# Reciprocal norms spread by transposes of their own column, and the last gated output of a chunk formed in PSUM

## The chip, the cores and the metric

The kernel runs on one core of a Trainium2 chip. The metric is device time in microseconds (us): the median over several timed executions of the whole program. A core has five engines with queues of their own, which run beside each other and wait for each other by semaphores: PE (TensorE, matrix products into PSUM), DVE (VectorE), ACT (ScalarE), POOL (GpSimd) and SP (SyncE, which mostly issues DMA transfers). SBUF is the on-chip memory that all engines read and write, with 128 partitions; PSUM holds 8 banks of 128 partitions × 512 fp32 values, in which PE leaves its results.

## The reference

A hybrid encoder with two layers: windowed grouped-query attention, then Fourier mixing, each behind an RMS norm, gated by SiLU, projected and added to the residual; a last norm follows. It is applied to a prompt of 2048 tokens and to a sample of 512 tokens, width 1024, 16 heads of 64, 4 key/value heads. The change concerns the attention layer alone:

```python
def rmsnorm(x, g):
    inv = lax.rsqrt(jnp.mean(x * x, axis=-1, keepdims=True) + RMS_EPS)
    return x * inv * g

def attention_layer(x, g, w_in, w_out, sink, rel_bias):
    h = rmsnorm(x, g)
    z = h @ w_in                      # q | k | v | gate
    ...
    o = banded_gqa_with_sink(q, k, v, rel_bias, sink)   # |i-j| <= 128, blocks of 128 queries
    return x + (o * jax.nn.silu(gate)) @ w_out
```

Everything is fp32. The kernel reaches that precision by splitting each operand of a product into a high part (fp32r) and a low part, the difference, and by three matmuls per product: high×high, high×low, low×high.

## The kernel before, in words

`matmul3` (L91–95) issues the three matmuls. `load_w` (L97) brings in a weight tile of 128×1024: in the first chunk from the input, with ACT casting the high part (L107) and POOL subtracting the low part in four pieces (L112) and a store of both to a buffer in DRAM, `wsd` (L116); in later chunks straight from that buffer.

`attention_phase` runs over five chunks of 512 own tokens: chunk 0 is the sample, chunks 1 to 4 are the prompt (chunks 1 to 3 with 128 tokens more as a halo). Activations lie transposed, channels over partitions and tokens along the free dimension. So the reciprocal norm of a token, which comes out as one value per partition (`inv`, tokens over partitions, a column for each block of 128 tokens), has to be laid along the free dimension and be the same on all 128 partitions. That is what `spread` does (L149–164). For up to four blocks at once, DVE forms `dg` = identity × the broadcast column of `inv` (L158, 128×512 fp32), PE multiplies it by a matrix of ones into a PSUM bank `ib` (L162), and ACT copies the bank to the SBUF tile `invb` (L163).

For each chunk:

- `make_h` (L166): loads `xT` by channel tile `xk`; POOL multiplies it by `invb` (L180); ACT forms the high part of `h` (L184) and DVE the low part (L185), both with the gain of the norm. Chunk 0 leaves the multiplication by `invb` out here, and scales the results of the products instead (`scaled`, L241).
- `kv_proj` (L244): K, then V. In chunk 0, whose norms come late, K's evacuation waits: `norms()` is called after K's products, V is evacuated with `inv` as a scale per token, and then `spread` (L312) precedes the scaled evacuation of K.
- `qg_proj` (L322): q and gate for each of 8 pairs of heads, `p`; the gate goes through tanh (L351) to `s` (L353).
- `attention` (L365): scores into one of two PSUM tiles `spt` (L396), bias and minimum (L408), exp (L412), scaling of `S` by the reciprocal sum (L418, in chunk 0 for half the heads on ACT, L421), transposes of `S` against the identity (L432) and their split into `pts` (L433, L434), the product with V into the bank `av` (L446), and `out_evac` (L451): ACT copies one half (`t2`, L454), DVE adds both heads' halves into an SBUF tile `o` (two adds, L457), `o` is multiplied by `s` (L461), ACT writes the high part of `uT` (L463), and the low part is subtracted (L464). L461 and L464 are on POOL, save for the last evacuation of a chunk (`p == 7`, blocks 2 and 3), where they are on DVE.
- `out_proj` (L468): two halves of 512 columns, four PSUM banks each; `uT` × the output weights, residual added by DVE (L516), stored (L517).

The main loop (L608–677) has 64 steps for the 8 pairs × 4 blocks × 2 heads, and five more to drain. Each step issues scores, the transposes of three steps earlier, the product with V of five steps earlier, and a share of the filling work, which is the q and gate projection of the next pair, or, in pair 7, the first half of the output projection. The statistics of the next chunk are taken from step 28 on, and `spread(c + 1, inv)` is called at step 56 (L650). What is left of the output projection (`tail`) runs with `make_h` of the next chunk.

What order an engine sees is not the order of the program text: a scheduler places each instruction in its engine's queue, and an engine works strictly in queue order, so that an instruction that waits holds everything behind it. PSUM has six general banks, given out in turn (`bank`), and the two `spt` tiles. A new use of a bank waits until its last reader is done.

Of the kernel before, what the change touches and what calls it, by code (L numbers as in the profile page):

```python
# [8 lines left out]
F32 = mybir.dt.float32  # L9
# [4 lines left out]
ALU = mybir.AluOpType  # L14
# [4 lines left out]
P = 128  # L19
# [19 lines left out]
def f32(ap):  # L39
    return ap.bitcast(F32)  # L40
# [3 lines left out]
def encoder(  # L44
# [3 lines left out]
    PE, ACT, DVE, POOL, SP = nc.tensor, nc.scalar, nc.vector, nc.gpsimd, nc.sync  # L48

    cpool = ctx.enter_context(tc.tile_pool(name="cpool", bufs=1))  # L50
# [6 lines left out]

    ident = cpool.tile([P, P], F32, name="ident")
    make_identity(nc, ident)
    ones = cpool.tile([P, P], F32, name="ones")  # L60
    DVE.memset(ones, 1.0)
    mhalf = cpool.tile([P, 8], F32, name="mhalf")
    POOL.memset(mhalf, -0.5)
    g0s = cpool.tile([P, KD], F32, name="g0s")
# [11 lines left out]
    def bank(name):  # L76
        return psum.tile([P, 512], F32, tag="bank", name=name)
# [13 lines left out]
    def matmul3(out, a, b, start, stop, more=False):  # L91

        PE.matmul(out, a[0], b[0], start=start, stop=False, skip_group_check=more)  # L93
        PE.matmul(out, a[0], b[1], start=False, stop=False, skip_group_check=more)  # L94
        PE.matmul(out, a[1], b[0], start=False, stop=stop, skip_group_check=more)  # L95
# [30 lines left out]
    def attention_phase():  # L126

        with ExitStack() as es:
            ap = es.enter_context(tc.tile_pool(name="attn", bufs=1))
# [16 lines left out]

                return [lambda i=i: one(i) for i in range(nt)] + [lambda: inv_rms(ss, nt, f"inv{c}")]

            def spread(c, inv):  # L149

                tok, lo_t, hi_t = CHUNKS[c]
                nt = min(640, hi_t - tok) // P
                invb = ap.tile([P, 640], F32, tag="invb", name=f"invb{c}")
                for i0 in range(0, nt, 4):
                    m = min(4, nt - i0)
                    ps = bank(f"ib{c}_{i0}")
                    dg = ap.tile([P, 4, P], F32, tag="tmp", bufs=2, name=f"dg{c}_{i0}")
                    DVE.tensor_tensor(  # L158
                        dg[:, :m], ident.unsqueeze(1).to_broadcast([P, m, P]),
                        inv[:, i0 : i0 + m].unsqueeze(2).to_broadcast([P, m, P]), ALU.mult,  # L160
                    )
                    PE.matmul(ps[:, : m * P], ones, dg[:, :m].rearrange("p i q -> p (i q)"), start=True, stop=True)  # L162
                    ACT.copy(invb[:, i0 * P : (i0 + m) * P], ps[:, : m * P])  # L163
                return invb

# [34 lines left out]
            ps = bank("idle")  # L200
# [25 lines left out]
            spt = []  # L226
            for i in range(2):
                s = spsum.tile([P, 512], F32, name=f"spt{i}")
# [15 lines left out]
            def kv_proj(c, hs, halo, norms=None, early=None):  # L244
                tok, lo_t, hi_t = CHUNKS[c]
                first = tok == lo_t
                own0 = 0 if first else P
                n = CH - own0
                if not first:
                    for g in range(4):  # L250
                        DVE.tensor_copy(kwin[g][:, :, 0:256], f32(kwin[g][:, :, 512:768]))
                inv = invb = None

                def evac_k(t, ps, n, wc):
                    ps = scaled(ps, invb, f"k{t}")
                    for j in range(2):
                        kw = kwin[2 * t + j]
                        sp = ps[j * 64 : j * 64 + 64, :n]
                        cs = slice(wc, wc + n)
                        for rows in (slice(0, 64), slice(64, 128)):  # L260
                            ACT.copy(kw[rows, 0, cs], sp)
                            DVE.tensor_tensor(kw[rows, 1, cs], sp, f32(kw[rows, 0, cs]), ALU.subtract)

                wk = early or [load_w(c, 8 + t, f"k{c}_{t}", DVE) for t in range(2)]

                def wslice(w, k, c0, n):
                    hi, lo = w[k // 4]
                    ks = slice((k % 4) * 256 + c0, (k % 4) * 256 + c0 + n)
                    return hi[:, ks], lo[:, ks]

                def cols(h, c0, n):
                    return h[0][:, c0 : c0 + n], h[1][:, c0 : c0 + n]

                kps = [bank(f"kp{c}_{t}")[:, :n] for t in range(2)]
                for k in range(KD):
                    for t in range(2):
                        matmul3(kps[t], wslice(wk, k, t * P, P), cols(hs[k], own0, n), k == 0, k == KD - 1)
                if halo:
                    ps = bank(f"kh{c}")[:, :256]
                    for k in range(KD):  # L280
                        matmul3(ps, halo[k], wslice(wk, k, 0, 256), k == 0, k == KD - 1)
                    kh = ap.tile([P, 256], F32, tag="tmp", bufs=2, name=f"kh{c}")
                    ACT.copy(kh, ps)
                wv = []
                if norms is not None:
                    wv.append(load_w(c, 10, f"v{c}_0", DVE))
                    inv = norms()
                else:
                    for t in range(2):
                        evac_k(t, kps[t], n, own0 + P)  # L290
                wv += [load_w(c, 10 + t, f"v{c}_{t}", DVE) for t in range(len(wv), 2)]
                blocks = [(hs, own0 + i * P, (tok + own0) // P + i) for i in range(n // P)]
                if halo:
                    blocks.append((halo, 0, tok // P + 4))
                for i0 in range(0, len(blocks), 4):
                    group = blocks[i0 : i0 + 4]
                    ps = [bank(f"vp{c}_{i0}_{i}")[:, :256] for i in range(len(group))]
                    for k in range(KD):
                        for i, (src, c0, b) in enumerate(group):
                            matmul3(ps[i], cols(src[k], c0, P), wslice(wv, k, 0, 256), k == 0, k == KD - 1)  # L300
                    for i, (src, c0, b) in enumerate(group):
                        v = ap.tile([P, 4, 2, HD], F32R, align_bytes=LINE, tag="v", bufs=6, name=f"v{c}_{b}")
                        vp = ps[i].rearrange("p (g d) -> p g d", g=4)
                        sc = 0.5
                        if inv is not None:
                            sc = ap.tile([P, 1], F32, tag="vsc", bufs=2, name=f"vsc{c}_{b}")
                            DVE.tensor_scalar(sc, inv[:, i : i + 1], 0.5, None, ALU.mult)
                        ACT.activation(v[:, :, 0, :], vp, AF.Copy, scale=sc)
                        DVE.scalar_tensor_tensor(v[:, :, 1, :], vp, sc, f32(v[:, :, 0, :]), ALU.mult, ALU.subtract)
                        vblk[b] = v  # L310
                if norms is not None:
                    invb = spread(c, inv)  # L312
                    for t in range(2):
                        evac_k(t, kps[t], n, own0 + P)
                if halo:
                    pt = bank(f"kht{c}")[:, :256]
                    for t in range(2):
                        PE.transpose(pt[:, t * P : t * P + P], kh[:, t * P : t * P + P], ident)
                        evac_k(t, pt[:, t * P : t * P + P], P, CH + P)
                return invb  # L320
# [44 lines left out]
            def attention(c, p, res, uTs):  # L365
# [3 lines left out]
                st = {}  # L369
# [81 lines left out]
                def out_evac(b):  # L451
                    ps = st["av"].rearrange("p (b h q) -> p b h q", b=2, h=2)
                    t2 = ap.tile([64, 2, 2, P], F32, tag="t2", bufs=1, name=f"t2{c}_{p}_{b}")
                    last_evac[0] = ACT.copy(t2, ps[64:128])  # L454
                    o = ap.tile([P, 2, P], F32, tag="o", bufs=2, name=f"o{c}_{p}_{b}")
                    for j in range(2):
                        DVE.tensor_tensor(o[64 * j : 64 * j + 64], ps[0:64, :, j], t2[:, :, j], ALU.add)  # L457
                    cs = slice((b - 1) * P, (b + 1) * P)
                    of = o.rearrange("p b q -> p (b q)")
                    eng = DVE if p == 7 and b == 3 else POOL  # L460
                    eng.tensor_tensor(of, of, res["s"][:, cs], ALU.mult)  # L461
                    uT = st["uT"]
                    ACT.copy(uT[:, 0, cs], of)  # L463
                    eng.tensor_tensor(uT[:, 1, cs], of, f32(uT[:, 0, cs]), ALU.subtract)  # L464

                return start, scores, transp, av, out_evac

# [140 lines left out]
            for c in range(len(CHUNKS)):  # L608
# [13 lines left out]
                res = [{} for p in range(8)]  # L622
# [5 lines left out]
                for i in range(64 + LAG + AVLAG):  # L628
                    p, n = divmod(i, 8)
# [14 lines left out]
                    if c + 1 < len(CHUNKS):  # L644
                        if i == 24:
                            norm_steps = stats(c + 1)
                        if i >= 28 and i % 4 == 0 and norm_steps:
                            inv = norm_steps.pop(0)()
# [657 lines left out]
```

## Time and profile before

| | |
|---|---|
| timed executions | 1682.95, 1677.16, 1679.39 us |
| median | 1679.39 us |
| profiled execution, its own time | 1680.38 us |
| profiled execution, span of the trace | 1678.6 us |
| granted PE clock, mean | 0.996 |
| PE / DVE / ACT / POOL busy | 98% / 70% / 52% / 23% |

In a line of the profile, L158 is line 158 of the kernel; then come the engine, the operation, the tiles (out <- in), the shape, and a count. In a timeline line the first number is the start in us from the start of the span, the second the busy time; brackets at the end give how long the engine had stood idle before and whose work ended that. Where a line counts several instructions, its time is that of the group. A matmul's duration includes its way through the array: the rate is read from the distance of two starts. In windows of time the granted clock is given as a share of full speed.

### The profile page before, as it was taken

Reading aid. Unit: us, or ns where it says so; the run is one execution under the profiler, and the core shown is the slowest. Engines: PE = TensorE matmul, PEld = TensorE weight load, DVE = VectorE, ACT = ScalarE, POOL = GpSimd, SP = SyncE. Lnnn points to the kernel's source line nnn. Section 1 sums busy time; section 2 is a strip of 40 time slices with the busy share of each in tenths; the row PEclk is TensorE's granted clock in tenths of the full one; section 3 lists DMA queues with packets and bytes.
Section 4 is the critical chain, followed back from the end, with each engine's and each line's share of the span. In section 5 each row is a group of like instructions: output and inputs, shape, how many; then the busy total and the mean of one; then the engine's idle time right before and its main releaser. Section 6 shows DMA issues by size and latency. Waiting matters only on the chain.

```text
span 1678.6 us, 25638 instructions
## 1 busy us (share of the span) xinstructions
PE 1648.0 (98%) x8980; PEld 1413.9 (84%) x8980; DVE 1182.3 (70%) x2782; ACT 874.6 (52%) x1998; POOL 392.1 (23%) x544
## 2 busy tenths in 40 slices
PE   9999899999999999999999999999999999999998
PEld 6887778888898888988888888888888887888886
DVE  5788645888638886478874588758676768888553
ACT  6788624676326674256752466646554455343321
POOL 2466740211403122221114211121112121111000
PEclk9999999999999999999999999999999999999999
DMA  8487775454765455763548644556556468453331
GB/s 306 154 330 308 262 285 207 167 197 161 261 226 186 174 185 180 272 223 132 183 151 318 250 151 164 212 199 221 190 205 236 171 229 338 158 194 126 122 126 51
DMA packets 91341, 344.69 MB, mean 205 GB/s; under 512 B 11163, under 2 KB 21403, under 8 KB 73292
## 3 DMA queue, kind: packets, MB, share of 16 engines
q1 hardware_dynamic: 73404, 267.79, 45.6%
q0 software_dynamic: 17520, 74.46, 11.3%
q8 instruction: 72, 1.18, 0.3%
q10 hardware_dynamic: 288, 0.79, 0.2%
q14 instruction: 57, 0.47, 0.1%
HBM read 267.47 MB, written 75.53 MB: 204 GB/s over the span
## 4 chain that ended last, share of the span: by engine, by line
PE 85%; DVE 5%; ACT 4%; DMA 3%; issue 2%; POOL 1%; SPq 0%; DVEq 0%; POOLq 0%; ACTq 0%
PE av L446 6%; PE spt L396 6%; PE pt L432 6%; PE qp L93 4%; PE qp L95 4%; PE qp L94 4%; PE gp L93 4%; PE gp L95 4%; PE gp L94 4%; PE op L93 4%; PE fo L94 4%; PE fo L95 3%; PE op L95 3%; PE op L94 3%; PE fo L93 3%; PE W L93 2%
## 5 line engine op out<-in xcount | busy, mean ns | idle before, releaser
L412 ACT ACTIVATE S<-S 128x385 f32<-128x385 f32 (+1 forms) x320 | 191.1, 597 | 40.5 <-DVE S L408 39.7
L433 ACT CAST pts<-pt 128x384 fp32r<-128x384 f32 (+1 forms) x320 | 144.6, 455 | 118.9 <-PE pt L432 114.5
L434 DVE TENSOR_TENSOR pts<-pt,pts 128x384 fp32r<-128x384 f32 (+1 forms) x320 | 168.6, 527 | 47.6 <-ACT pts L433 44.3
L408 DVE CUSTOM_DVE_ANT_0 S<-spt,b 128x385 f32<-128x385 f32 (+1 forms) x320 | 168.9, 528 | 37.0 <-PE spt L396 32.1
L396 PE MATMUL spt<-kwin,qab 128*128 128x384 f32 (+1 forms) x640 | 158.7, 329 | 1.6 <-DVE S L408 1.6
L461 POOL TENSOR_TENSOR o<-o,s 128x256 f32<-128x256 f32 x75 | 55.4, 738 | 429.5 <-DVE o L457 423.3
L432 PE MATMUL pt<-ident,S 128*128 128x128 f32 x896 | 150.5, 274 | 0.0
L396 PEld LDWEIGHTS spt<-kwin,qab 128*128 128x128 f32 x640 | 119.0, 188 | 29.4 <-DVE S L408 2.7
L446 PEld LDWEIGHTS av<-pts,v 128*128 128x128 f32 x896 | 126.7, 189 | 16.0 <-DVE pts L434 3.1
L446 PE MATMUL av<-pts,v 128*128 128x256 f32 x896 | 136.6, 285 | 2.9 <-DVE pts L434 2.0
L93 PE MATMUL qp<-h,wq 128*128 128x512 f32 x320 | 137.2, 429 | 0.7 <-ACT wq L107 0.7
L93 PE MATMUL gp<-h,wg 128*128 128x512 f32 x320 | 137.8, 431 | 0.0
L418 DVE TENSOR_SCALAR S<-S 128x384 f32<-128x384 f32 (+1 forms) x288 | 129.9, 451 | 8.5
L93 PE MATMUL op<-wo,uT 128*128 128x512 f32 x320 | 127.0, 398 | 2.9 <-ACT uT L463 2.9
L93 PE MATMUL fo<-wo,tTu 128*128 128x512 f32 x320 | 125.8, 393 | 1.3 <-ACT wo L1108 1.3
L432 PEld LDWEIGHTS pt<-ident,S 128*128 128x128 f32 x896 | 114.2, 140 | 14.7 <-DVE pts L434 3.4
L95 PE MATMUL qp<-h,wq 128*128 128x512 f32 x320 | 126.2, 394 | 0.1
L94 PE MATMUL op<-wo,uT 128*128 128x512 f32 x320 | 125.9, 394 | 0.0
L95 PE MATMUL gp<-h,wg 128*128 128x512 f32 x320 | 125.8, 393 | 0.0
L94 PE MATMUL qp<-h,wq 128*128 128x512 f32 x320 | 125.8, 393 | 0.0
L94 PE MATMUL gp<-h,wg 128*128 128x512 f32 x320 | 125.7, 393 | 0.0
L94 PE MATMUL fo<-wo,tTu 128*128 128x512 f32 x320 | 125.4, 392 | 0.1
(341 smaller groups left out, 4113.8 us busy)
## 6 DMA issues: line engine op xcount, KB each, us to landing
wq<-wsd SPq DMA_DIRECT2D x32, 1024.0 KB, 4.8
wg<-wsd SPq DMA_DIRECT2D x32, 1024.0 KB, 5.6
wo<-wsd SPq DMA_DIRECT2D x32, 1024.0 KB, 4.9
x<-x1d SPq DMA_DIRECT2D x40, 512.0 KB, 3.7
b<-b21d SPq DMA_DIRECT2D x40, 512.0 KB, 5.9
b<-rowd SPq DMA_DIRECT2D x40, 384.0 KB, 4.2
xs<-in_x_dram SPq DMA_DIRECT2D x23, 512.0 KB, 6.6
s2d<-gt POOLq DMA_DIRECT2D x40, 256.0 KB, 4.1
```

The costliest lines, as they stand in the source:

```text
L93: PE.matmul(out, a[0], b[0], start=start, stop=False, skip_group_check=more)
L94: PE.matmul(out, a[0], b[1], start=False, stop=False, skip_group_check=more)
L95: PE.matmul(out, a[1], b[0], start=False, stop=stop, skip_group_check=more)
L396: PE.matmul(ps[:, 2 + k0 * P : 2 + k1 * P], q, kwin[g][:, part, b * P + k0 * P : b * P + k1 * P], start=part == 0, stop=part == 1,)
L408: DVE.tensor_tensor_reduce(out=s[:, e0:e1], in0=ps[:, 1 + e0 : 1 + e1], in1=st["bias"][:, j, 386 - e1 : 386 - e0][:, ::-1], scale=1.0, sca ...
L412: last_exp[0] = ACT.activation(s[:, e0:e1], s[:, e0:e1], AF.Exp, bias=mn, scale=-1.0, accum_out=den)
L418: DVE.tensor_scalar(s[:, ks], s[:, ks], den, None, ALU.mult)
L432: PE.transpose(ps[:, kb, :], s[:, 1 + kb * P : 1 + (kb + 1) * P], ident)
L433: ACT.copy(hi[:, k0:k1, j, :], ps[:, k0:k1, :])
L434: DVE.tensor_tensor(lo[:, k0:k1, j, :], ps[:, k0:k1, :], f32(hi[:, k0:k1, j, :]), ALU.subtract)
L446: PE.matmul(out, v, pt[:, kb].rearrange("p h q -> p (h q)"), start=kb == k0 and part == 0, stop=kb == k1 - 1 and part == 1,)
L461: eng.tensor_tensor(of, of, res["s"][:, cs], ALU.mult)
```

## The change

Three things are changed.

First, `spread` no longer forms `dg`, and the matrix of ones is dropped. PE transposes the column of `inv` of each block, broadcast along the free dimension to 128×128, against the identity; four such transposes fill a bank, which ACT copies to `invb` as before.

Second, in chunk 0 `spread` is called inside the loop over V's products, after the fifth of eight channel tiles, and writes to the second `spt` tile instead of a general bank. DVE then sets that tile to zero, as the scores expect it. K's scaling can follow at once.

Third, in the last `out_evac` of a chunk, `o` is not an SBUF tile but the half of the `av` bank in which the first operand lies: the two adds write it in place, the product with `s` and the subtraction of the high part run on it on DVE, and ACT reads the high part from it. The bank is free only after the subtraction. All other evacuations are as before.

```diff
-    ones = cpool.tile([P, P], F32, name="ones")
-    DVE.memset(ones, 1.0)
...
-            def spread(c, inv):
+            def spread(c, inv, place=None):
...
-                    ps = bank(f"ib{c}_{i0}")
-                    dg = ap.tile([P, 4, P], F32, tag="tmp", bufs=2, name=f"dg{c}_{i0}")
-                    DVE.tensor_tensor(
-                        dg[:, :m], ident.unsqueeze(1).to_broadcast([P, m, P]),
-                        inv[:, i0 : i0 + m].unsqueeze(2).to_broadcast([P, m, P]), ALU.mult,
-                    )
-                    PE.matmul(ps[:, : m * P], ones, dg[:, :m].rearrange("p i q -> p (i q)"), start=True, stop=True)
+                    ps = bank(f"ib{c}_{i0}") if place is None else place
+                    for i in range(m):
+                        PE.transpose(ps[:, i * P : (i + 1) * P], inv[:, i0 + i : i0 + i + 1].to_broadcast([P, P]), ident)
                     ACT.copy(invb[:, i0 * P : (i0 + m) * P], ps[:, : m * P])
...
                             matmul3(ps[i], cols(src[k], c0, P), wslice(wv, k, 0, 256), k == 0, k == KD - 1)
+                        if norms is not None and k == 4:
+
+                            invb = spread(c, inv, spt[1])
+                            DVE.memset(spt[1], 0.0)
...
                 if norms is not None:
-                    invb = spread(c, inv)
                     for t in range(2):
                         evac_k(t, kps[t], n, own0 + P)
...
-                    o = ap.tile([P, 2, P], F32, tag="o", bufs=2, name=f"o{c}_{p}_{b}")
+                    cs = slice((b - 1) * P, (b + 1) * P)
+                    uT = st["uT"]
+                    if p == 7 and b == 3:
+
+                        o, eng = ps[:, :, 0], DVE
+                    else:
+                        o, eng = ap.tile([P, 2, P], F32, tag="o", bufs=2, name=f"o{c}_{p}_{b}"), POOL
                     for j in range(2):
                         DVE.tensor_tensor(o[64 * j : 64 * j + 64], ps[0:64, :, j], t2[:, :, j], ALU.add)
-                    cs = slice((b - 1) * P, (b + 1) * P)
-                    of = o.rearrange("p b q -> p (b q)")
-                    eng = DVE if p == 7 and b == 3 else POOL
-                    eng.tensor_tensor(of, of, res["s"][:, cs], ALU.mult)
-                    uT = st["uT"]
-                    ACT.copy(uT[:, 0, cs], of)
-                    eng.tensor_tensor(uT[:, 1, cs], of, f32(uT[:, 0, cs]), ALU.subtract)
+                    s, hi, lo = (t.rearrange("p (b q) -> p b q", b=2) for t in (res["s"][:, cs], uT[:, 0, cs], uT[:, 1, cs]))
+                    eng.tensor_tensor(o, o, s, ALU.mult)
+                    ACT.copy(hi, o)
+                    eng.tensor_tensor(lo, o, f32(hi), ALU.subtract)
```

Line numbers of the changed file differ from those of before by a few: the transposes are at L156, the copy to `invb` at L157, the memset of `spt` at L298, the adds of `out_evac` at L460, the product with `s` at L462, the high part at L463 and the low part at L464.

The instruction order that the build gives each engine also moves. On PE the transposes of a spread directly follow the last gate matmul of that pair; at a chunk's end 17 instead of 14 matmuls of the second half's earlier banks stand between the last product with V and the matmuls that need the last `uT`. On DVE at a chunk's end the first residual add (L516 before) now stands between the two adds of `out_evac` or between them and the product with `s`; in chunk 0 the low part of `h` of the next chunk (L185) stands ahead of the low part of `uT`. On ACT in chunk 0 the high part of the next chunk's second `h` stands ahead of the high part of `uT`. POOL and SP only swap neighbouring transfers.

## The prediction

> **What bounds the kernel now.** I read the page's engine rows and chain first, then the PE groups, then every operation on the tile `dg` (the spread), then the timeline around each spread and each chunk end.
>
> ```profile
> span 1678.6 us, 25638 instructions
> PE 1648.0 (98%) x8980; PEld 1413.9 (84%) x8980; DVE 1182.3 (70%) x2782; ACT 874.6 (52%) x1998; POOL 392.1 (23%) x544
> PE 85%; DVE 5%; ACT 4%; DMA 3%; issue 2%; POOL 1%; SPq 0%; DVEq 0%; POOLq 0%; ACTq 0%
> ```
>
> PE is busy 98% of the span and carries 85% of the chain that ended last. So a gain must come from PE work that goes, or from the few places where PE stands still. The 5% of DVE and 4% of ACT in the chain are such places. The spread makes one of them, in the timeline of chunk 0 (start, duration, engine, in brackets the wait before it):
>
> ```profile
> 177.49 4.03 DVE L158 TENSOR_TENSOR dg<-ident,inv 128x512 f32<-128x512 f32 x1
> 177.51 3.46 POOL L112 TENSOR_TENSOR wo<-w32o,wo 128x256 fp32r<-128x256 f32 x5
> 177.63 0.62 PE L396 MATMUL spt<-kwin,qab 128*128 128x384 f32 x2 [1.61 <-DVE S L408]
> 177.79 1.05 ACT L107 CAST wo<-w32o 128x1024 fp32r<-128x1024 f32 x1 [1.03 <-DMA wsd<-wlate]
> 181.67 2.04 PE L162 MATMUL ib<-dg,ones 128*128 128x512 f32 x2 [3.43 <-DVE dg L158]
> ```
>
> The product `dg` takes 4.03 us here and about 0.68 elsewhere; it ends as POOL's run of five weight pieces ends. PE waits 1.61 and then 3.43 us, and after the second wait its granted clock is low, as the busy time by windows shows (window, length, busy PE, PEld, DVE, ACT, POOL with counts, clock, DMA share, GB/s):
>
> ```profile
> 181.60:187.30 5.70, 5.63 (x15) 4.30 (x16) 3.98 (x15) 2.69 (x9) 3.45 (x6) 0.50 0.99 383
> 187.30:195.00 7.70, 7.70 (x44) 6.52 (x42) 2.60 (x9) 4.26 (x11) 4.49 (x8) 1.00 0.96 335
> ```
>
> The second place is the end of chunk 0 (same timeline columns):
>
> ```profile
> 213.34 0.58 ACT L454 COPY t<-av 64x512 f32<-64x512 f32 x1 [2.90 <-PE av L446]
> 213.96 4.58 POOL L180 TENSOR_TENSOR xk<-xk,invb 128x640 f32<-128x640 f32 x3
> 215.50 3.32 DVE L461 TENSOR_TENSOR o<-o,s 128x256 f32<-128x256 f32 x1
> 218.86 0.40 ACT L463 CAST uT<-o 128x256 fp32r<-128x256 f32 x1 [2.27 <-DVE o L461]
> 219.32 0.50 PE L93 MATMUL op<-wo,uT 128*128 128x512 f32 x1 [2.85 <-ACT uT L463]
> 219.34 0.41 DVE L464 TENSOR_TENSOR uT<-o,uT 128x256 fp32r<-128x256 f32 x1
> ```
>
> The gate product at L461 lasts 3.32 us while POOL multiplies `xk`, and 0.42 at the other four chunk ends; PE waits 2.85 for what follows. Two more lines price the rest, a regular spread and the longest row of `h`'s low part:
>
> ```profile
> 410.43 1.10 PE L162 MATMUL ib<-dg,ones 128*128 128x512 f32 x2
> ...
> 449.43 5.62 DVE L185 SCALAR_TENSOR_TENSOR h<-xk,g0s,h 128x512 fp32r<-128x512 f32 x1 [1.20 <-ACT h L184]
> ```
>
> The row of L185 normally takes 0.74; here POOL multiplied `xk` from 449.25 to 454.49. So a DVE product with both inputs in SBUF is held for a whole POOL run. DVE rows that read PSUM were not held: at 214.02 two adds took 0.42 each (L457) and at 214.90 the residual add 0.69 (L516), in the same POOL run that held L461.
>
> **A. First chunk.** The fp32 product `ones`×`dg` holds PE for four passes of a 512-column matmul, 4×0.2263 (the steady start-to-start) = 0.905 us. It is replaced by four transposes; a transpose starts every 0.108 in the score runs, so 0.43. In the trace `ib` stands at 33.27, just before the first `qp`, and `qp` waits for a bank until about then in both versions (ACT empties V only after its cast of `wq`, 31.27 to 32.32). PE waits 1.4 us before `ib`, so four transposes put earlier, among V's matmuls, are absorbed. −0.9. `inv` is ready at 23.11 and PE reaches the new place at about 26, so PE does not wait; the added memset of `spt` on DVE (estimate 0.5 from 512-column rows) and the copy on ACT at about 28 lie in idle time before ACT's 31.27 cast. Bounds: 0 if something else holds `qp` as long, −2.4 if the 1.40 wait goes too.
>
> **B. Spread for chunk 1 (176 to 189 us).** What goes: waits of 1.61 and 3.43, half a clock over 181.60–187.30 (5.63 busy, so 2.8), and 1.13 of `ib` (0.905, plus 0.226 for its 128 columns) against 0.54 for five transposes, 0.59. Together 8.4. The transposes follow the last `gp` matmul at about 175.5, where `inv` has long been there. What is late next: the first out-projection matmul takes the bank that `ib` leaves, and that bank is free only when ACT has copied to `invb`. ACT's cast of a weight waits for a DMA until 177.79 and ends at 178.84; tanh (0.59) and the copies (0.59, 0.27) follow, so about 179.9. PE runs out of other work at about 178.2: a new wait of 1.7. The copies also stand ahead of the next exp, 0.5. So −8.4 + 1.7 + 0.5 = −6.2. Removing `dg` takes DVE's two rows (4.03, 0.28) away; the score sums queue behind nothing new. Bounds: −3 if PE still loses its clock and DVE's scaling of S (usually 0.34, 2.37 at 138.51 and 2.42 at 158.87 under POOL runs) is held in its place; −7.5 if the new wait is nearly nothing.
>
> **C. End of chunk 0.** With `o` in PSUM the gate product reads PSUM and SBUF; by the L457 and L516 rows it is not held: about 0.42 for 3.32. But the new order moves other work ahead. On ACT the high part of `uT` now stands behind `h1_1`, which waits for POOL's second `xk` product: 4.85 us after the `t` copy starts, 5.92 before. On DVE the low part stands behind the low part of `h1_0`, both inputs in SBUF, which by the 5.62 row is held until POOL's run ends; the low part is done at about 6.35, 6.41 to 6.54 before. PE gets three more out-projection matmuls (plus one) before it needs it, 4×0.2263 = 0.9. So −1.1, not −2.9. Bounds: −2.9, the whole 2.85 wait; +1 if `h1_0` is held 5.62 and not 4.6.
>
> By the Trainium skill, "SBUF — State Buffer", section "SBUF: two separate sides", the engine that comes first has the shared port pair "for the whole instruction", and a DVE op with two SBUF inputs would be held for one POOL instruction alone. The 4.03 us under five pieces of 0.69 speaks against it. By the page `h1_0` would be held for one 1.53 us product and C would be about −2.9, the sum −12.5.
>
> **D. Spreads for chunks 2 to 4** (409, 633, 857 us). POOL is idle and nothing is held. PE saves 1.13−0.54 = 0.59 twice and, with four blocks, 0.905−0.43 = 0.47: 1.65. PE also starts `ib` 0.28 late each time (410.03 to 410.43 for a matmul of 0.12), as it waits for `dg`: 0.84. −2.5. Bounds: −3.3 if every excess of those stretches goes (some 0.55 each beside `ib`'s own); +0.7 if a transpose costs its row's mean duration, 0.274: 5×0.274 = 1.37 against 1.13.
>
> **E. Ends of chunks 1 to 3, F. end of chunk 4.** The residual add (0.62 to 0.69) moves ahead of the gate product, so `uT` comes about 0.63 later; three more out-projection matmuls (0.7) stand in front of it. PE waits 0.2 there now. 0, ±0.6 each. At the last end nothing of this size moves: 0. The dropped `ones` (one memset at the start) and SP's swapped `xk` load cost nothing: chunk 1's `h` is ready at 242 for a product at 250, 8 us of cover; were it gone, the 4.58 run would show.
>
> **Sum.** −0.9 −6.2 −1.1 −2.5 = −10.7. The profiled execution took 1680.38, 1.0 above the median 1679.39; so 1669.7 beside it, 1668.7 as a median.
>
> **Rivals.**
> 1. *The gain at chunk 1's spread is given back.* POOL's pieces stay, so DVE's S scaling is held in `dg`'s place, and ACT's cast waits for its DMA; PE stops long enough to lose its clock again. B = −3, C = 0, A = 0, D = −1.65: about −4.7, 1674.7. For it: the 2.37 and 2.42 rows, and a wait of 1.61 already there. Against: PE has some 2 us of other work.
> 2. *More.* The new wait in B is short and C's `h1_0` is free: −7.5, −2.9, −0.9, −2.5 = −13.8, 1665.6.
> 3. *Slower: the chunk ends run into POOL.* At the ends of chunks 1 to 3 DVE's low part of `h` now stands ahead of the gate product or `uT`'s low part. POOL's `xk` runs end at 440.38, 664.69 and 887.66, the low parts begin at 442.57, 666.85 and 890.93. If the `xk` run moves 2.2 us later against the chunk's end, each is held as at 449.43: 3×(5.62−0.75) = +14.6, net +4, 1683.3. Against: `xk` moves with the copy of the out evacuation, so with the end.
> 4. *The change does not do what it says*: a transpose of a broadcast column takes 0.274 or PE waits for `inv`. A = 0, D = +0.7, B still −5, C −1.1: −5.4, 1674.0. No trace here has such a transpose; L432's 0.108 start-to-start is from ordinary ones.
>
> **How the numbers follow.** My forecast 0.46; rival 1 0.14, rival 2 0.18, rival 4 0.10, rival 3 0.12. About 0.3%, 5 us, is what a measurement of this kernel can tell from no change. Forecast and rival 2 are faster (0.64); of rivals 1 and 4, which end at −4.7 and −5.4, half: 0.12, so 0.76. Same: their other half, 0.12, and 0.02 of rival 3's milder forms. Slower 0.10. Range: 1664 (rival 2 and its bounds) to 1677 (rivals 1 and 4, and a part held); about a tenth is left out above, a tenth below.
>
> **What will show it.** Right: no `dg` rows; after 176 us no PE wait above 2 us and clock 1.0 throughout 176–190 (B); the row at L460 of the new file about 0.42 at chunk 0's end, and the low part of `h1_0` long, not the gate product (C); five transposes in about 0.6 near 408, 632, 856 (D). Wrong: a low clock after chunk 1's spread, L185 rows of 4 to 6 us at the ends of chunks 1 to 3, PE waiting on `invb`'s copy for over 3 us.

## The result and the profile after

The changed kernel takes 1667.25 us (median of six, 1666.17 to 1668.19), the kernel before 1679.38 on the same chip: 0.9926 of it, 95% interval 0.9913 to 0.9939, 12.1 us less. Forecast were 1668.7 and 10.7 us less. The profiled execution's span is 1666.0 us, 12.6 below that of before.

Page lines (span, busy engines, chain by engine) of the changed kernel:

```profile
span 1666.0 us, 25639 instructions
PE 1643.4 (99%) x8987; PEld 1413.4 (85%) x8987; DVE 1173.1 (70%) x2774; ACT 874.2 (52%) x1998; POOL 391.3 (23%) x544
PE 86%; ACT 4%; DVE 4%; DMA 3%; issue 1%; POOL 1%; SPq 0%; DVEq 0%; POOLq 0%; ACTq 0%
```

PE's busy time fell by only 4.6 us (1648.0 to 1643.4), the span by 12.6: most of the gain is PE standing still less. PE runs at half clock for 10.2 us in both traced executions, the last microseconds of the program aside (6.8 and 3.4 before, three times 3.4 after). All operations on the spread's bank, in the changed kernel (count, then least, median and longest duration in ns):

```profile
L156 PE MATMUL ib<-ident,inv x19: 271/272/273, 174.4 to 847.8; 128*128 128x128 f32 x19
L157 ACT COPY invb<-ib x7: 277/576/581, 179.1 to 848.1; 128x512 f32<-128x512 f32 x4, 128x128 f32<-128x128 f32 x3
```

The nineteen transposes take 272 ns each from start to end, as those of the scores do (274 before): a column broadcast as their input costs nothing more. At the spread for chunk 1 the timeline after reads:

```profile
174.43 0.71 PE L156 MATMUL ib<-ident,inv 128*128 128x128 f32 x5
...
177.27 3.47 POOL L110 TENSOR_TENSOR wo<-w32o,wo 128x256 fp32r<-128x256 f32 x5
...
177.62 1.05 ACT L105 CAST wo<-w32o 128x1024 fp32r<-128x1024 f32 x1 [1.10 <-DMA wsd<-wlate]
178.57 0.59 ACT L348 ACTIVATE th<-gp 128x512 f32<-128x512 f32 x1
179.06 0.74 ACT L157 COPY invb<-ib 128x512 f32<-128x512 f32 x2
...
179.69 0.79 PE L91 MATMUL op<-wo,uT 128*128 128x512 f32 x1 [1.51 <-ACT invb L157]
```

The five transposes start 0.109 us apart, so 0.54 in all, where `ib` held PE for 1.13 of full-speed time. PE's new wait is 1.51 us, and ACT's copy ends it, behind the cast that waits for a DMA: the step that the prediction named as late next, at 1.7. The clock is not in the sum; the bound of −3 and the first rival had it. By windows (length, busy times, granted clock, DMA share, GB/s):

```profile
175.97:179.38 3.41, 1.72 (x11) 1.15 (x9) 1.82 (x7) 2.31 (x5) 3.09 (x6) 1.00 0.69 181
179.40:182.80 3.40, 3.11 (x7) 2.48 (x8) 3.15 (x10) 3.35 (x12) 2.29 (x4) 0.50 1.00 395
```

It is halved for 3.4 us after the shorter wait, where before it was halved for 6.8. The end of chunk 0 after:

```profile
208.80 4.60 POOL L174 TENSOR_TENSOR xk<-xk,invb 128x640 f32<-128x640 f32 x3
...
210.88 0.43 DVE L462 TENSOR_TENSOR av<-av,s 128x256 f32<-128x256 f32 x1
...
211.22 2.74 DVE L179 SCALAR_TENSOR_TENSOR h<-xk,g0s,h 128x512 fp32r<-128x512 f32 x1
...
212.69 0.37 ACT L463 CAST uT<-av 128x256 fp32r<-128x256 f32 x1
...
213.12 0.50 PE L91 MATMUL op<-wo,uT 128*128 128x512 f32 x1 [1.03 <-ACT uT L463]
...
213.88 0.41 DVE L464 TENSOR_TENSOR uT<-av,uT 128x256 fp32r<-128x256 f32 x1
...
214.35 0.50 PE L93 MATMUL op<-wo,uT 128*128 128x512 f32 x1 [0.27 <-DVE uT L464]
```

The gate product in PSUM takes 0.43 where it was held for 3.32; now the low part of `h` is held, 2.74, with the low part of `uT` behind it. PE waits 1.03 and 0.27 for 2.85.

To place the gain, each matmul of a trace is paired with the same one of before (same tiles, same count), and the lead is how much earlier it starts. The table gives how much the lead grows at each place, in us, in the traced execution of several kernels. "Before again" is the unchanged kernel traced once more, and so shows what executions differ by; "spread only" and "PSUM only" are the first two runs of the next section.

| place (time of before) | after | after, repeated | before again | spread only | PSUM only |
|---|---|---|---|---|---|
| A, first chunk, to 60 us | 0.07 | 0.66 | 0.16 | 0.86 | -0.55 |
| the same, had the `wq` cast begun at 31.27 | 0.83 | 0.86 | 0.02 | 0.84 | 0.01 |
| B, spread for chunk 1 | 4.83 | 5.87 | 0.95 | 5.71 | 0.89 |
| C, end of chunk 0 | 1.34 | 1.35 | -1.65 | -1.35 | 1.22 |
| V of chunk 1 (256) | 0.85 | 0.86 | 0.86 | 0.86 | 0.57 |
| D, three later spreads | 2.51 | 2.51 | -0.54 | 2.53 | -0.10 |
| E, ends of chunks 1 to 3 | 0.72 | 0.66 | 0.06 | 0.05 | 0.68 |
| start of the Fourier phase (1130) | 2.10 | 2.14 | 2.00 | 1.91 | 2.27 |

From 1200 us to the end the lead changes by −0.2, +0.5, −0.2, −1.6 and +0.1 in these five traces. All of them but before again are at half clock for 3.4 us somewhere between 1387 and 1412, where the two traces of before are not.

### The profile page after: what moved, and what is told of

The parts are those of the page before. It is cut to its first block, busy times and chain, and to the rows that moved or that the text cites. A ratio compares the mean times of both kernels' runs of the same rounds, so it can differ in the third digit from the quotient of the medians.

```text
span 1666.0 us, 25639 instructions
## 1 busy us (share of the span) xinstructions
PE 1643.4 (99%) x8987; PEld 1413.4 (85%) x8987; DVE 1173.1 (70%) x2774; ACT 874.2 (52%) x1998; POOL 391.3 (23%) x544
## 4 chain that ended last, share of the span: by engine, by line
PE 86%; ACT 4%; DVE 4%; DMA 3%; issue 1%; POOL 1%; SPq 0%; DVEq 0%; POOLq 0%; ACTq 0%
PE av L443 6%; PE spt L393 6%; PE pt L429 5%; PE qp L91 4%; PE qp L93 4%; PE op L91 4%; PE qp L92 4%; PE op L93 4%; PE gp L91 4%; PE gp L93 4%; PE op L92 4%; PE gp L92 4%; PE fo L92 3%; PE fo L93 3%; PE fo L91 3%; PE W L91 2%
## 5 line engine op out<-in xcount | busy, mean ns | idle before, releaser
L462 POOL TENSOR_TENSOR o<-o,s 128x256 f32<-128x256 f32 x75 | 55.3, 737 | 425.7 <-DVE o L460 425.6
```

The costliest lines, as they stand in the source:

```text
L462: eng.tensor_tensor(o, o, s, ALU.mult)
```

## The experiments

**The parts by themselves.** Spread only: the changed kernel with the last evacuation as before.

```diff
-                    if p == 7 and b == 3:
-                        o, eng = ps[:, :, 0], DVE
+                    o = ap.tile([P, 2, P], F32, tag="o", bufs=2, name=f"o{c}_{p}_{b}")
+                    eng = DVE if p == 7 and b == 3 else POOL
```

> The changed kernel with the last evacuation of a chunk as it was before (o in SBUF), so only the two parts on the spread. If the parts add up as read from the traces, it keeps about 5.0 us at the spread for chunk 1 and 2.5 at the three later spreads and gives back about 1.2 at the end of chunk 0 and 0.6 at the ends of chunks 1 to 3: about 1669 us, with the gate product held for 3 us or more at chunk 0's end and PE waiting 2.5 to 3 us there. The rival, that the end of the chunk costs the same whatever holds it, gives 1667 us. Open: the 2.1 us at the start of the Fourier phase; if they come from the spread they stay, otherwise the time is about 1671.

Measured: 1671.61 us (0.9951 of before, 0.9932 to 0.997), 2.6 more than the sum of parts said. The product is held again, as timeline lines of this run show:

```profile
209.02 3.32 DVE L458 TENSOR_TENSOR o<-o,s 128x256 f32<-128x256 f32 x1
...
212.84 0.80 PE L91 MATMUL op<-wo,uT 128*128 128x512 f32 x1 [2.84 <-ACT uT L460]
```

PE waits 2.84, and here the wait also costs the clock, which is half for 3.4 us from 212.8 on (C is -1.35 in the table). So the wait at C is dearer than its length where the clock falls: it did so too in before again and in the last run below, not in the first trace of before nor in the run before the last. In no traced run with the product in PSUM is the clock low there. The 2.1 us of the Fourier phase are there, although the time is that of the branch without them: C's clock and the 1.6 us lost after 1200 us make it so. The rival (1667) fell.

PSUM only: the kernel before with the edit above the other way round.

> The kernel before with only the last evacuation of a chunk formed in PSUM. By the sum of parts: 1.2 us at the end of chunk 0 and 0.6 at three others, about 1677.5 us; dg still takes 4 us at 177 and PE waits 1.6 and 3.4 us there. If the 2.1 us at the start of the Fourier phase come from this part, about 1675.5. The rival, that low parts of h now queue ahead and cost more than the gate product gives, gives 1679 or more.

Measured: 1675.35 us (0.9977, 0.9967 to 0.9987). C and E gain 1.22 and 0.68, as in the changed kernel; A, B and D nothing that before again does not show. The rival, that the low parts of `h` cost more than is gained, fell. That the time is 2.1 below the first expectation is not the Fourier phase, which moved in every run; in before again C costs 1.65 more by the clock, and this part takes that away.

**The place in the first chunk.** The changed kernel with the spread behind V's evacuation, in a general bank.

```diff
-                        if norms is not None and k == 4:
-                            invb = spread(c, inv, spt[1])
-                            DVE.memset(spt[1], 0.0)
...
                 if norms is not None:
+                    invb = spread(c, inv)
                     for t in range(2):
```

> The changed kernel with chunk 0's spread back behind V's evacuation, into a general bank, still by transposes. If the first q products start when ACT has emptied V behind its weight cast, the place is worth at most the 0.43 us of four transposes: 1667.2 to 1667.7 us, and the first q product starts as late as in the changed kernel. If my step on the first chunk was right in that the fp32 product's time went, the place is worth 0.4 to 0.9. The rival, that the early K scaling shortens the path, gives 1668.5 or more.

Measured: 1669.1 us (0.9942, 0.9921 to 0.9963). By its time this is the rival's run, that K's early scaling shortens the path; but the interval can't tell 0.4 us, and the trace does not show such a path. The `wq` cast begins at 31.81 here, 0.54 later than before, and the lead at 60 us is -0.13: 0.41 had the cast begun at 31.27, against 0.83 to 0.86 with the early place. So the place is worth 0.43, which is four transposes at 0.108, and the other 0.41 to 0.43 of A is the fp32 product that became transposes (0.905 to 0.43). B, C and V gain 5.84, 1.34 and 0.87, as in the repeated trace. What makes this execution slower lies after 1200 us, where it loses 1.4, with half clock from 1384.0 and again from 1401.1; whether the late place has a part in that is not shown.

**The same kernels traced again.** The changed kernel, unedited:

> The changed kernel once more, for another trace of it. If the half clock after the spread for chunk 1 follows from PE's wait for ACT's copy, it is there again, at about the same place and for about 3.4 us. If it hangs on where a measuring window falls, it is gone or moved, here or at the start of the Fourier phase, and the time at those two places differs by up to 1.5 us each. The start of the first matmuls will differ by a microsecond or so; if the first q product is set by ACT and its DMA, PE's wait before it takes that up.

Measured: 1666.21 us (1665.58 to 1670.65 in three executions). It waits as long as in the first trace, and the clock stays whole. Timeline and windows:

```profile
179.59 0.50 PE L91 MATMUL op<-wo,uT 128*128 128x512 f32 x1 [1.58 <-ACT invb L157]
```

```profile
177.39:180.80 3.41, 1.83 (x8) 1.34 (x9) 1.54 (x7) 3.26 (x8) 3.41 (x6) 1.00 0.94 299
179.40:182.80 3.40, 3.21 (x15) 2.61 (x15) 3.12 (x11) 3.35 (x12) 2.22 (x4) 1.00 0.99 388
```

The same wait is followed by 15 matmuls in 3.4 us and not 7, which is worth 1.0 us in B. What differs is where the wait falls. In every trace the stretches of half clock begin whole multiples of 3.413 us apart: in the first trace of the changed kernel at 8.71, 179.38 and 1401.35, which is 50 and 358 steps. Laid over the wait, that grid gives the windows 175.97–179.38 there and, reckoned back from 1399.36, 177.39–180.80 here; PE was busy 1.72 us of the one and 1.83 of the other. The order run below had 1.80 (174.10–177.51) and lost the clock after a wait of 1.36; spread only had 2.12 (175.21–178.62) and the late place 2.24 (179.11–182.52) and kept it, after longer waits of 1.78 and 1.65. A limit does not follow from this: later in the program a window with 1.64 busy (order, 1379.01–1382.41) did not cost the clock, and one with 2.14 (before, 1125.98–1129.38) did.

The kernel before, unedited:

> The kernel before once more, for another trace. If the 2.1 us at the start of the Fourier phase belong to the change, the wait of 0.58 us ahead of the second row of transposes and the half clock after it are here again. If they hang on where a measuring window falls, the half clock of 3.4 us is gone or elsewhere and the stage is 1.4 us shorter; the wait of 0.58 would stay. After the held dg the low clock must come again in any case, as PE stands still for 5 us in 5.7.

Measured: 1679.3 us. After the held `dg` the clock is half for 6.8 us again. At the start of the Fourier phase the wait of 0.58 is gone and the clock whole, in windows of this run and of before:

```profile
1129.40:1132.80 3.40, 3.40 (x31) 3.40 (x30) 3.40 (x7) 3.07 (x7) 0.00 (x0) 1.00 0.95 342
```

```profile
1129.40:1132.80 3.40, 3.40 (x18) 3.40 (x17) 2.90 (x6) 2.33 (x5) 0.00 (x0) 0.50 0.92 334
```

So 2.0 of the 2.1 us there belong to that one execution of before, not to the change. The unchanged kernel paid elsewhere in this execution: half clock from 219.6 (C, -1.65).

**The two waits left.** Order: on DVE the low part of the last `uT` ahead of the next `h`, and on ACT its high part.

```diff
+                    if c == 1:
+                        after(dn, last_u[1])      # dn: DVE low part of h or hl
+                        if k:
+                            after(up, last_u[0])  # up: ACT high part of h or hl
...
-                    ACT.copy(hi, o)
-                    eng.tensor_tensor(lo, o, f32(hi), ALU.subtract)
+                    last_u[0] = ACT.copy(hi, o)
+                    last_u[1] = eng.tensor_tensor(lo, o, f32(hi), ALU.subtract)
```

> The changed kernel with one change of order at the end of chunk 0: on DVE the low part of the last uT comes ahead of the low parts of the next chunk's h, on ACT its high part ahead of those from the second channel tile on. If those two kept PE waiting there (1.03 and 0.27 us in the changed kernel), both waits go and PE gains about 1.2 us by the end of chunk 0; the held low part of h then costs nothing, as its product is 8 us off. About 1666 us. The rival, that the gate product or ACT's copy sets the end there anyway, leaves the wait and the time.

Measured: 1667.37 us, no gain on the changed kernel (1666 was expected). The two waits are gone: C gains 3.07 against 1.34. But V of chunk 1 gives 0.99 back where the changed kernel gains 0.85. The timeline of this run at V:

```profile
243.15 0.69 DVE L525 TENSOR_TENSOR xr<-xr,op 128x512 f32<-128x512 f32 x1 [8.35 <-DMA xr<-in_x_dram]
244.46 1.18 ACT L264 CAST kwin<-kp 64x512 fp32r<-64x512 f32 x2 [1.95 <-DVE kwin L265]
...
246.99 0.37 ACT L286 COPY kh<-kh 128x256 f32<-128x256 f32 x1
...
247.42 0.39 PE L91 MATMUL vp<-wv,h 128*128 128x256 f32 x1 [1.58 <-ACT kh L286]
```

DVE's last residual add of chunk 0 waits for its load; K's low parts stand behind it on DVE, ACT's K casts behind those, the copy that frees V's bank behind the casts. In before PE waited behind the same chain:

```profile
256.42 0.39 PE L93 MATMUL vp<-wv,h 128*128 128x256 f32 x1 [0.63 <-ACT kh L283]
```

DVE copy: `invb`'s copies for chunk 1 on DVE.

```diff
-                    ACT.copy(invb[:, i0 * P : (i0 + m) * P], ps[:, : m * P])
+                    (DVE.tensor_copy if c == 1 else ACT.copy)(invb[:, i0 * P : (i0 + m) * P], ps[:, : m * P])
```

> The changed kernel with invb's two copies for chunk 1 on DVE and not on ACT. If PE's 1.51 us wait before the first output-projection matmul comes from ACT's queue (its weight cast waits for a DMA), PE no longer waits there and the stage gains 1.2 to 1.5 us, and up to 1.4 more in executions where the wait cost the clock. About 1665.5 us. The rival, that DVE is held by POOL's pieces also for a copy from PSUM, shows a copy of 2 us or more and PE waits as long.

Measured: 1666.73 us, where 1665.5 was expected. B grows by 6.02, 0.15 more than in the repeated trace. The wait moved:

```profile
176.47 0.88 DVE L157 COPY invb<-ib 128x512 f32<-128x512 f32 x2
...
177.34 1.05 ACT L105 CAST wo<-w32o 128x1024 fp32r<-128x1024 f32 x1 [1.26 <-DMA wsd<-wlate]
...
178.29 0.59 ACT L348 ACTIVATE th<-gp 128x512 f32<-128x512 f32 x1
178.99 0.69 DVE L350 SCALAR_TENSOR_TENSOR s<-th,gp 128x512 f32<-128x512 f32 x1 [1.30 <-ACT th L348]
...
179.73 0.50 PE L91 MATMUL op<-wo,uT 128*128 128x512 f32 x1 [0.87 <-DVE s L350]
```

PE starts the output projection 2.4 us earlier than in the repeated trace (177.21) and stops at its next bank, which the gate leaves after tanh, and tanh stands behind the same cast. The copies were not held by POOL (0.88 for both), so the run's rival fell. Both edits together:

> Both edits together. If they act at separate places, 2.4 to 3 us below the changed kernel, about 1664.5 us, and 0.991 of the kernel before. The rival, that the time so won is taken back before the fourth chunk, since the weights' casts and the next chunk's h come no sooner, leaves 1666 to 1667 us.

Measured: 1667.08 us (0.9936, 0.9922 to 0.9949): the rival's number. C gains 3.14, V loses 1.01.

Both, and a tile of its own for the load in question:

```diff
-                            xt = residual(half, i, res_tile.pop(0) if res_tile and i == 3 else None)
+                            own = c == 0 and half == 1 and i == 3
+                            xt = residual(half, i, ap.tile([P, 512], F32, tag="tmp", bufs=2, name="xrt") if own else
+                                          res_tile.pop(0) if res_tile and i == 3 else None)
```

> Both edits, and a tile of its own for the last residual of chunk 0, so that its load need not wait for an earlier tile. If what is won at the end of chunk 0 is lost at chunk 1's V because DVE's last residual add waits for that load with K's low parts queued behind it (PE waited 1.74 to 1.81 us there with the order edits, not at all in the changed kernel), the wait at V is gone and the gain of the order stays: 1.7 us below the run with both edits, about 1665 us. The rival, that the next chunk's h or ACT's K casts set V's start, leaves a wait of 1 us or more and the same time.

Measured: 1664.59 us (0.9915, 0.9901 to 0.9928), 2.5 below both and 2.7 below the changed kernel by medians, though the intervals overlap. The two traced executions took the same time (1664.03 with both, 1663.98 here): the one with both won 1.9 us elsewhere, in A, in the Fourier phase and at the very end. C gains 3.12, V 0.86, and K's casts run without a break:

```profile
240.40 3.92 ACT L264 CAST kwin<-kp 64x512 fp32r<-64x512 f32 x6 [8.64 <-PE kp L93]
```

So the load's tile was what took C's gain back at V; that the program gains by it is likely, not shown. The tile alone, in the changed kernel:

> The changed kernel with only the tile of its own for that residual. PE does not wait at chunk 1's V in the changed kernel, so nothing is to be had: 1667 us, within 0.5. If the load's early place on SP delays an output weight or the next xk, PE waits longer at the end of chunk 0 and the time is a microsecond or more above.

Measured: 1666.18 us (0.9922, 0.9907 to 0.9937), C 1.31 and V 0.86 as without it: nothing is gained at these places, as expected. The time is 0.8 below the expected 1667, within the scatter of its executions.

**How long POOL holds DVE.** In the kernel before, POOL's pieces of some weights halved.

```diff
-            for i in range(4):
-                cs = slice(i * 256, i * 256 + 256)
+            m = 128 if n in (22, 23) else 256
+            for i in range(D // m):
+                cs = slice(i * m, i * m + m)
```

> The kernel before, with the low part of two output weights formed in eight pieces of 128 columns and not four of 256, on POOL. If a DVE product with two SBUF inputs is held until POOL's whole run of pieces ends, dg again takes about 4 us at 177. If it is held for one instruction alone, it takes 0.7 plus at most one piece of about 0.4, so 1.1 us or less, and PE's 3.43 us wait shrinks to under 1.

Measured: 1677.4 us in one run. It does not settle the question, since the halved pieces came later; but `dg` took 2.69 (177.15 to 179.84) and ended before POOL's run (176.50 to 180.15) did. With the pieces at the right place (21 and 22 in the list):

> The kernel before, with the low parts of the second and third output weight in eight pieces of 128 columns on POOL, the second being the one under which dg is held. In the run named pieces the halved pieces came only after 182 us, and dg got in ahead of the fifth whole piece (2.69 us). If POOL keeps the way to SBUF for its whole run, dg takes 3 us or more again; if the way is open between two pieces and DVE takes it now and then, dg is shorter, the earlier the more joints there are: 0.7 to 2.7 us. Held for one piece alone, 1.1 us.

Measured: 1679.04 us in one run.

```profile
177.67 4.33 POOL L113 TENSOR_TENSOR wo<-w32o,wo 128x128 fp32r<-128x128 f32 x9
178.32 0.79 DVE L159 TENSOR_TENSOR dg<-ident,inv 128x512 f32<-128x512 f32 x1
179.25 1.10 PE L163 MATMUL ib<-dg,ones 128*128 128x512 f32 x2 [0.19 <-DVE dg L159]
```

In the midst of nine pieces `dg` takes 0.79: it got in at a joint, and POOL's third piece took 0.91 beside it where the others took 0.44 to 0.50. So it is not held for a run as such, and PE's 3.43 wait is 0.19. Yet B is only 1.64 here, 0.69 more than in before again: PE still waits 2.2 before the score product ahead, another 0.57 behind `ib`, and the clock is half for the same 6.8 us. So the hold alone was not what the spread cost. The rest went with the transposes: the place in PE's queue, where everything behind the product waits for a chain over DVE, and the clock lost by that. No run moves the old product alone, so this share is argued from what is left.

## Why the prediction was right, point by point

- **A, -0.9.** Right in size (0.83 to 0.86, half from the product, half from the place), once the start of ACT's cast of `wq`, which waits for a DMA, is taken out; the cast begins at 29.5 to 32.0 in the traced runs, so one execution shows the gain or not. The three traces in which it begins after 31.8 are those with half clock from about 8.5 to 12; that one causes the other is not shown. The bounds of 0 and -2.4 were needed for that.
- **B, -6.2.** 4.83 and 5.87. The wait of 1.7 came as 1.51 and 1.58 from the releaser that was named. The step "half a clock over 181.60–187.30" was taken to go whole; in one of the two traces 3.4 us of it came back after the new wait, which is the difference of 1.0. That is the prediction's own sign of being wrong ("a low clock after chunk 1's spread"), and the forecast of a full clock from 176 to 190 holds for one trace of two. Before again spends 0.95 less here than the first trace of before; against it B is 3.9 and 4.9.
- **C, -1.1.** 1.34, by the steps foreseen: the `uT` high part is done 4.89 us after the copy starts (forecast 4.85), the low part 6.12 (6.35). The step that failed is the cause given for the hold: "a DVE product with both inputs in SBUF is held for a whole POOL run". In the last two runs it was not (2.69 and 0.79). C came out because at this place the low part of `h` was in fact held to the end of POOL's run: it stood from 211.22, POOL's products ended at 211.91 and 213.40, and it was done at 213.96, so it did not get in at the first of these joints. The prediction set the Trainium skill's page "SBUF — State Buffer", section "SBUF: two separate sides", aside on this. By that section of the Trainium skill the port pair is taken for one instruction, and the 0.79 agrees with it; the 2.74 here and the 4.03 under five whole pieces do not, if DVE enters at the next joint. When it does was not settled.
- **V of chunk 1: not in the sum.** That "chunk 1's `h` is ready at 242 for a product at 250" was true and beside the point: the bound was a residual load in the same queue chain, which took 1.0 in the order runs. The 0.85 of the changed kernel is not its own: before again shows 0.86 with nothing changed, after losing 1.65 at C.
- **D, -2.5.** 2.51. Both terms, shorter products and the late start, were right.
- **E, 0.** -0.7, inside the bounds: three more matmuls in front cover the residual add and the old 0.2 us wait as well.
- **F.** Some 0.15, where 0 was forecast; the 2.1 us nearby belong to the traced execution of before.
- **Rivals.** 1: S's scaling was 0.35 to 1.00 and not 2.4; its low clock came in one trace of two, for 3.4 us and not 6.8. 2: the new wait was 1.51 and `h1_0` was held for 2.74, so neither of its conditions came. 3: one such row came, L179 with 5.55 us at 665.03, but PE's wait at the ends of chunks 1 to 3 shrank. 4: the transposes cost 0.109 from start to start.

The sum came out within 1.5 us, and part of that is luck: by the time alone the second rival (1665.6) is almost as near as the forecast, and only the steps decide against it. The places shift with the execution of before that is taken as the base: from before again to the repeated trace B is 4.9, C 3.0, V 0, D 3.05, E 0.6, A 0.5 and the Fourier phase 0.1, in sum much the same. In one execution of before the clock was lost at the Fourier phase, in the other at C; the forecast had neither, and it had too much in B and too little in E.

## What to carry to other kernels

What an operation blocks in an in-order queue costs more than the operation: replacing a 0.9 us product by 0.43 us of transposes gained some 0.4 us where the product was not late (A), and four to six where it stood in front of ready work and waited for another engine (B). When a wait goes, look for the next holder of the same resource: here a bank (copy, then tanh), and some 30 us later a load whose tile came free late, which took the whole gain of the order back. Trace the unchanged kernel twice before assigning a few microseconds to a change.

## What the runs showed of the hardware that was not expected

- The low clock comes in stretches of 3.4 us or twice that in every trace, the last one aside, in which the program ends. In each trace their starts lie on one grid of 3.413 us. A full such stretch of standing still is not needed: in the changed kernel PE was busy 1.72 of the 3.41 us before 179.38. The Trainium skill's page "TensorE: Matmul & The Clock Gate", Part 1, gives a window of about 3.4 us, which agrees, and one idle window as the condition, which these runs do not bear out.
- The same instructions with waits of 1.51 and 1.58 us lost the clock in one execution and not in the other, and waits of 2.84 to 2.87 at C cost it in three traces of five: where one window of the grid was left with 0.66 to 1.05 us of busy PE (spread only, pieces at the right place, before again), not where two windows shared the wait and each had 1.84 or more (before, the run with the later pieces). So a wait of 1.4 to 3 us (1.36 in the order run) has a price of its length plus 1.0 to 1.7 us now and then, by where it falls on that grid.
- A DVE product of two SBUF inputs took 0.79, 2.69, 3.38 and 4.03 us at the same place, by how POOL's pieces fell around it. The gate product of 128x256 took 3.32 us with both inputs in SBUF and 0.43 with one of them in PSUM, both times beside POOL's products on `xk`.
